# MLP weight sums made early and kept in HBM, and seven products in the first piece's second column group

## The chip, the cores and the metric

The kernel runs on one core of a Trainium2 chip. A core has a matrix engine, TensorE (PE), and three engines for the rest: VectorE (DVE), ScalarE (ACT) and GpSimd (POOL). Each takes its instructions in the order in which they stand in its queue. SyncE (SP) and POOL issue the transfers between HBM and the core's memory. The metric is the time of one execution on the device in microseconds (us); lower is better.

## What is computed

One layer of a decoder trunk, on 256 tokens with 16 meta tokens ahead of them, model width 2048, all in float32:

```python
u = rms_norm(h, g_pre_mix[l])
proj = u @ w_in[l]                       # 2048 x (1024 + 1024 + 1024 + 2048 + 2048)
z_pool, v_conv, g_conv, gate_a, gate_b = jnp.split(proj, splits, axis=-1)
y_a = causal_multiscale_pool(z_pool, w_pool_grp[l], pool_scale[l]) @ w_pool_out[l]
y_b = conformer_conv(v_conv, g_conv, w_dw[l], b_dw[l], conv_ln_g[l], conv_ln_b[l]) @ w_conv_out[l]
m = jax.nn.sigmoid(gate_a) * y_a + jax.nn.sigmoid(gate_b) * y_b
h = h + rms_norm(m @ w_o[l], g_post_mix[l])
u = rms_norm(h, g_pre_mlp[l])
f = jnp.square(jax.nn.relu(u @ w_up[l])) @ w_down[l]     # 2048 -> 8192 -> 2048
h = h + rms_norm(f, g_post_mlp[l])
return h[:, N_META:]
```

The convolution is a causal depthwise one with 31 taps, followed by a layer norm over channels and a swish.

## The kernel before

**Weights.** Every weight matrix passes once from HBM, in chunks of 1 MB: 128 partitions by 2048 float32. A chunk is split into a high part, a cast on ACT (`hi`, line 276), and a low part, a subtraction on DVE (`lo`, line 279). Each product is then three matmuls: high by high, high by low, low by high. Three buffers stand behind the raw chunks and three behind the parts. `fetch()` hands the next chunk to PE; before that it opens the chunks up to two ahead (its load on SP, then its cast and subtraction), and it flushes what was put off for ACT (`late`).

**Stages.** The order of the program is: the start, with x loaded in blocks (`x_in`) that PE transposes (line 434); the projection by w_in, which first makes the convolution's value and gate (to about 107 us), then the pool's input z (to 153 us), then the two gates (16 chunks each, to 327 us; matmuls at line 839); the pool and convolution outputs; w_o; and the MLP from about 505 us to the end. While PE works on w_in, DVE makes the 240 tap steps of the convolution (line 559), which `drain` puts between the chunks by a fixed budget of time for each. The gates' sigmoids are written by ACT (line 868) into two tiles `sg`, one for each gate, in rooms with the tags `s0` and `s1`. The room `s1` holds z before that. POOL has little to do: it sets some constants at the start and, between 377 and 390 us, brings sums of w_o blocks with four loads (`early_sums`, line 921), two of which add to what stands in the core's memory.

**The MLP.** It runs in 8 pieces of 1024 hidden columns (NP = 8). In each, w_up's product is made (steps `U`: half h, pair a or b, part 0 or 1), then relu and square, and then w_down's product, whose weights are 2 by 4 blocks: two halves of the hidden columns by four column blocks of 512. The blocks B11, B12, B21, B22 are the first column group, X1 to X4 (Y in the last piece) the second. For two halves of tokens, two halves of hidden columns and two column blocks, eight block products would be needed; the steps P1 to P7 (first group) and Q1 to Q7 (second group) do with seven, each on a sum or difference of activations (`forms`) and a sum of weight blocks. One block product is 12 matmuls of 128x512. In the first piece's second group the steps X1 to X4 make the eight plain products; in the last piece all sixteen are plain.

Weight sums come in two ways. A load on POOL can add to what stands in a buffer (a *bring*, line 1603): before P1 it adds B12 to B11, at `add:P` it adds B22 to B12 for P7, and likewise in the second group. Or DVE adds two raw buffers in place (line 1598): for P6, P4, Q6 and Q4.

**The order of the MLP.** The strings of steps fix the order on PE and with it the order of loads on SP. The class `Plan` lists the work of all engines with a cost each (a bring on POOL 5.5 us, and 4.0 more until its data are there) and orders ACT, DVE and POOL by when PE needs what they make. The step R makes the row sums of a diagonal (`diag`, line 1638) from which `rb`, the tokens' scale, is copied (line 1923); activations of the first piece (line 1690) and `u` itself (line 1653, four pieces) are scaled by it.

Of the kernel before, what the change touches and what calls it, by code (L numbers as in the profile page):

```python
# [8 lines left out]
F32 = mybir.dt.float32  # L9
# [6 lines left out]
P = 128  # L16
CK = 4
CW = 512
# [97 lines left out]
def hybrid_block(ctx: ExitStack, tc: tile.TileContext, ins: dict, out: bass.AP):  # L116
    nc = tc.nc
    x = ins["x"][0]
    meta = ins["meta"]
    T, D = x.shape  # L120
    M = meta.shape[0]
    L = M + T
    NT = T // P
# [9 lines left out]
    w_down = ins["w_down"][0]  # L133
# [10 lines left out]
    big = ctx.enter_context(tc.tile_pool(name="big", bufs=1))  # L144
# [147 lines left out]
    def split_pieces(c):  # L292
        while opened[c][2]:
            opened[c][2].pop(0)()

    def fetch(ahead=2):

        for c in range(ahead + 1):
            if c == len(opened) and at["n"] < len(stream):
                open_chunk()  # L300
            if c < len(opened):
                split_pieces(c)
        flush()
        return opened.pop(0)[:2]
# [360 lines left out]
    def tap_columns():  # L665
# [194 lines left out]
    def block(n):  # L860
        return slice(n * CW, (n + 1) * CW)
# [4 lines left out]
    def evac_gate(b, n):  # L866
        def f(t, acc):
            late.append(lambda: nc.scalar.activation(sg[b][:, t, block(n)], acc, AF.Sigmoid,
                                                     scale=sc["r"][:, t:t + 1]))
        return f  # L870

    for b in range(2):
        sg[b] = big.tile([P, NT, D], F32, tag=f"s{b}", name=f"sg{b}")
        for n in range(NB):
            project_t(u_of, KD, evac_gate(b, n), f"gate{b}{n}", fill=2.9)

# [594 lines left out]
    plan = Plan()  # L1471
    FIRST_PIECE = "U1a0 U1a1 U1b0 R U1b1"
    PIECE = "U1b1"
    PLAIN = "X3 P1 U0a0+ X1 U0a1+ X4 U0b0+ U0b1+ U1a0+ P5 add:P P6 U1a1+ P3 X2 P7 U1b0+ P4 P2"
    BLOCKS = "P1 U0a0+ U0a1+ Q1 P5 P6 add:P P3 P7 P2 P4 Q5 U0b0+ U0b1+ Q3 Q6 add:Q U1a0+ U1a1+ Q7 U1b0+ Q2 Q4"
    MODES = [PLAIN] + [BLOCKS] * (NP - 2)
    LAST_PIECE = "Y1 U1b1 X1 Y3 Y2 Y4 X2 X3 X4"
    steps = []
    for i in range(NP):
        text = ((FIRST_PIECE if i == 0 else PIECE) + " " + MODES[i] if i < NP - 1 else  # L1480
                LAST_PIECE)
        steps += [(s[:-1], i + 1) if s[-1] == "+" else (s, i) for s in text.split()]
# [4 lines left out]
    col_halves = [slice(h * HALF_CW, (h + 1) * HALF_CW) for h in range(2)]  # L1487
    RAW_OF = {"P1": "B11", "P5": "B11", "P6": "B11", "P4": "B11", "P3": "B22", "P7": "B12",
              "P2": "B21", "Q1": "X1", "Q5": "X1", "Q6": "X1", "Q4": "X1", "Q3": "X4",
              "Q7": "X3", "Q2": "X2"}  # L1490
# [240 lines left out]
    def into_forms(h, pr, i, s_name, box):  # L1731
        G, A, ks = forms[h], f"A{h}{pr}", slice(2 * pr, 2 * pr + 2)

        n = 2 if h or i == NP - 1 or "X1" in MODES[i] else 1

# [128 lines left out]
    def product_block(m_, s, i):  # L1864
        h, f = FORM[s]
        bank = bank_of(s)
        start = s[1] in "65" or bank not in begun and bank != "zq2"
        begun.add(bank)
# [237 lines left out]
```

## Time and profile before

| | |
|---|---|
| median of 3 runs | 1184.26 us (1184.18 to 1184.5) |
| span of the profiled execution | 1183.2 us |
| PE busy | 1172.7 us |
| DVE busy | 1012.7 us |
| ACT busy | 680.7 us |
| POOL busy | 46.9 us |
| HBM read, written | 267.68 MB, 4.19 MB |
| mean rate of the transfers | 231 GB/s |

The profiled execution gives its span, from its first instruction to its last; the times of the runs are 1 us longer than that span. A row of the timeline names the start, the busy time, the engine, the line, the operation, what it writes and reads, the shape, how many instructions there are, and in brackets the idle time of the engine ahead of it with what ended that. A window row gives the busy time of each engine in a stretch. A row of the chain of waits gives start, length, and what ran.

### The profile page before, as it was taken

The page shows a single profiled execution, that of the slowest core. Times are in us where ns is not written, and L with a number is a line of the kernel's source. Part 1 is how long each engine was busy: PE and PEld are TensorE (multiplying, and loading weights), DVE is VectorE, ACT ScalarE, POOL GpSimd, SP SyncE. Part 2 cuts the span into 40 slices and gives each one's busy share as a digit, 9 for nine tenths or more (in the row PEclk, how much of TensorE's full clock was granted, in tenths as well). Part 3 has the DMA queues.
Part 4 walks back from the last instruction along what each step waited for, and adds up shares of the span by engine and source line. Part 5 has one row for each costly group of instructions (what it writes and reads, how often), then busy time and mean ns, then how long its engine had stood idle before and what let it go on. Part 6 is the DMA issues. An engine that isn't in the chain of part 4 may idle for free.

```text
span 1183.2 us, 15773 instructions
## 1 busy us (share of the span) xinstructions
PE 1172.7 (99%) x6351; PEld 1019.0 (86%) x6351; DVE 1012.7 (86%) x1094; ACT 680.7 (58%) x691; POOL 46.9 (4%) x52
## 2 busy tenths in 40 slices
PE   9999999999999999999999999999999999999996
PEld 9999988888888888898888888888888888888886
DVE  6899989986665799987998988989989989889865
ACT  6543344445654466756566766666756667666642
POOL 1000000000000001000001001000000010010000
PEclk9999999999999999999999999999999999999999
DMA  8655555655556967859868899898998998998861
GB/s 295 214 178 179 185 199 186 197 195 183 183 203 228 269 215 221 290 166 318 252 210 238 232 293 232 249 276 226 281 294 220 264 276 230 280 244 249 288 214 72
DMA packets 177882, 272.91 MB, mean 231 GB/s; under 512 B 4657, under 2 KB 92785, under 8 KB 176912
## 3 DMA queue, kind: packets, MB, share of 16 engines
q1 hardware_dynamic: 160176, 235.95, 58.8%
q0 software_dynamic: 16736, 34.76, 16.3%
q10 hardware_dynamic: 896, 1.19, 0.3%
q8 instruction: 50, 0.82, 0.3%
q14 instruction: 24, 0.20, 0.0%
HBM read 267.68 MB, written 4.19 MB: 230 GB/s over the span
## 4 chain that ended last, share of the span: by engine, by line
PE 99%; DMA 0%; DVE 0%; SPq 0%; issue 0%; DVEq 0%; ACT 0%; ACTq 0%
PE bank_u L498 18%; PE acc_gate L839 15%; PE bank_a L1802 10%; PE bank_u L504 9%; PE acc_up L1802 8%; PE bank_b L1802 7%; PE o_c L1185 6%; PE acc_z L493 4%; PE acc_co L839 4%; PE acc_po L839 4%; PE acc_v L493 3%; PE acc_g L493 3%; PE acc_vg L493 2%; PE acc_up L498 1%; PE bank_u L1802 1%; PE o_b L1185 1%
## 5 line engine op out<-in xcount | busy, mean ns | idle before, releaser
L498 PE MATMUL bank_u<-m,hi 128*128 128x512 f32 x960 | 329.4, 390 | 0.0
L504 PE MATMUL bank_u<-m,lo 128*128 128x256 f32 x960 | 265.5, 277 | 0.0
L276 ACT CAST hi<-raw 128x2048 fp32r<-128x2048 f32 (+2 forms) x94 | 151.1, 1620 | 187.2 <-PE acc_gate L839 37.6
L279 DVE TENSOR_TENSOR lo<-raw,hi 128x2048 fp32r<-128x2048 f32 (+2 forms) x94 | 180.2, 1927 | 60.5 <-ACT hi L276 60.1
L498 PEld LDWEIGHTS bank_u<-m,hi 128*128 128x128 f32 x960 | 180.2, 188 | 37.9
L1585 DVE TENSOR_TENSOR lo<-raw_m,hi 128x2048 fp32r<-128x2048 f32 x70 | 160.3, 2289 | 31.8 <-ACT hi L1581 31.7
L504 PEld LDWEIGHTS bank_u<-m,lo 128*128 128x128 f32 x960 | 180.3, 188 | 1.4
L1581 ACT CAST hi<-raw_m 128x2048 fp32r<-128x2048 f32 x70 | 133.9, 1913 | 74.2 <-DVE raw_m L1598 21.3
L839 PE MATMUL acc_gate<-hi,u_um 128*128 128x512 f32 x416 | 131.1, 389 | 0.0
L559 DVE SCALAR_TENSOR_TENSOR c<-a,taps,c 128x256 f32<-128x256 f32 x240 | 98.8, 485 | 0.1
L1802 PE MATMUL bank_a<-hi,forms 128*128 128x512 f32 (+1 forms) x288 | 93.6, 386 | 0.0
L839 PEld LDWEIGHTS acc_gate<-hi,u_um 128*128 128x128 f32 x416 | 78.1, 188 | 16.1
L839 PE MATMUL acc_gate<-lo,u_um 128*128 128x512 f32 x208 | 80.9, 389 | 0.0
L1581 ACT CAST hi<-raw_a 128x2048 fp32r<-128x2048 f32 x29 | 55.4, 1910 | 35.3 <-PE bank_u L498 13.8
L1585 DVE TENSOR_TENSOR lo<-raw_a,hi 128x2048 fp32r<-128x2048 f32 x29 | 66.4, 2289 | 10.8 <-ACT hi L1581 10.7
L1581 ACT CAST hi<-raw_c 128x2048 fp32r<-128x2048 f32 x27 | 51.5, 1908 | 27.3 <-PE bank_u L498 11.8
L1585 DVE TENSOR_TENSOR lo<-raw_c,hi 128x2048 fp32r<-128x2048 f32 x27 | 61.8, 2288 | 5.2 <-ACT hi L1581 5.1
L1802 PEld LDWEIGHTS bank_a<-hi,forms 128*128 128x128 f32 x288 | 53.9, 188 | 11.0
L1585 DVE TENSOR_TENSOR fourth_pair<-raw_m,fourth_pair 128x2048 fp32r<-128x2048 f32 x26 | 59.5, 2288 | 4.4 <-ACT fourth_pair L1581 4.4
L1665 ACT COPY half<-bank_u 128x256 f32<-128x256 f32 x60 | 22.2, 371 | 65.7 <-PE bank_u L504 65.7
L1802 PE MATMUL acc_up<-hi,forms 128*128 128x512 f32 x176 | 57.4, 390 | 0.0
L1802 PE MATMUL bank_a<-lo,forms 128*128 128x512 f32 (+1 forms) x144 | 55.6, 386 | 0.0
(421 smaller groups left out, 2268.2 us busy)
## 6 DMA issues: line engine op xcount, KB each, us to landing
raw<-in_w_in_dram SPq DMA_DIRECT2D x52, 1024.0 KB, 5.0
raw_m<-in_w_down_dram SPq DMA_DIRECT2D x38, 1024.0 KB, 6.8
raw_m<-in_w_down_dram POOLq DMA_DIRECT2D x22, 1024.0 KB, 10.2
raw_a<-in_w_up_dram SPq DMA_DIRECT2D x20, 1024.0 KB, 6.2
raw_c<-in_w_up_dram SPq DMA_DIRECT2D x19, 1024.0 KB, 7.2
raw_m<-in_w_up_dram SPq DMA_DIRECT2D x19, 1024.0 KB, 6.5
raw_a<-in_w_down_dram SPq DMA_DIRECT2D x13, 1024.0 KB, 6.9
raw_c<-in_w_down_dram SPq DMA_DIRECT2D x13, 1024.0 KB, 7.3
```

The source lines that it names most:

```text
L276: nc.scalar.copy(hi[:, sl, cs], raw[:, sl, cs])
L279: nc.vector.tensor_sub(lo[:, sl, cs], raw[:, sl, cs], f32(hi[:, sl, cs]))
L493: nc.tensor.matmul(acc, w[:, k[0], cs], act[:, k[1], a, off:], start=first and n == 0, stop=last and n == 2)
L498: nc.tensor.matmul(acc.rearrange("p (a t) -> p a t", a=2)[:, :, ts], hi[:, k[0], cs], act[:, k[1], :, off + ts.start:off + ts.stop], start ...
L504: nc.tensor.matmul(acc[:, :T], lo[:, k[0], cs], act[:, k[1], 0, off:], start=False, stop=stop, skip_group_check=True)
L559: nc.vector.scalar_tensor_tensor(c, conv["a"][:, q, i:i + T], taps[:, q, i:i + 1], c, op0=ALU.mult, op1=ALU.add)
L839: nc.tensor.matmul(acc, act(kk)[:, a_, ts_], w_[:, k, :], start=kk == 0 and n == 0, stop=kk == nk - 1 and n == 2)
L1185: nc.tensor.matmul(acc, form(k, a_), box[w_][:, k, :], start=start and k == 0 and n == 0, stop=stop and k == CK - 1 and n == 2, skip_group ...
L1581: nc.scalar.copy(box["hi"], raw)
L1585: nc.vector.tensor_sub(box["lo"], raw, f32(box["hi"]))
L1665: nc.scalar.copy(box[j], accs[j][:, :T])
L1802: nc.tensor.matmul(acc, forms[h][:, f, k, a_, :], box[w_][:, k, cs], start=start and k == 0 and n == 0, stop=stop and k == KH - 1 and n == ...
```

## The change

**Seven sums made early.** A generator, `second_sums`, takes a room of two chunks, loads the blocks B12 and B22 of a piece into it with two loads on POOL, adds them on DVE three fetches later and stores the sum with POOL in HBM (`early_t`). Every `fetch` first runs its next step. Pieces 0 to 3 use the room `s0` from the first fetch on, one piece every five fetches; pieces 4 to 6 use the room `s1`, in the gate stage, one every four. The tile of a gate's sigmoids is now made when the first of them is put off, in the same rooms, once the generator has run out. In the MLP, P7's weights are then a plain load from `early_t`.

**Seven sums by adding transfers.** `add:P` now adds B21 to B11 for P4, by a bring, where a DVE sum stood. In all there are 28 brings rather than 26, and 21 DVE sums rather than 26.

**Seven products in the first piece.** Its second group runs Q1 to Q7 instead of X1 to X4. That is one block product of 12 matmuls fewer.

**Another order of the steps.** R stands one up product earlier, and the strings of the pieces are new: one for the first piece, one for odd and one for even pieces, one for the last.

```diff
+    EARLY_SUMS = 7
+    early_t = dram.tile([P, EARLY_SUMS, CK * CW], F32, name="early_t")
+    beside = []
+    def second_sums(tag, pieces, gap):
+        room = big.tile([P, 2, CK * CW], F32, tag=tag, name=f"second_{tag}")
+        for i in pieces:
+            for h in range(2):
+                nc.gpsimd.dma_start(room[:, h].rearrange("p (k c) -> p k c", k=CK),
+                                    columns(w_down, (2 * i + h) * CK, CK, CW)[0][0])
+            yield from [None] * 3
+            nc.vector.tensor_add(room[:, 0], room[:, 0], room[:, 1])
+            nc.gpsimd.dma_start(early_t[:, i], room[:, 0])
+            yield from [None] * gap
+    def beside_step():
+        if beside and next(beside[0], True):
+            beside.pop(0)
     def fetch(ahead=2):
+        beside_step()
...
+    beside.append(second_sums("s0", range(0, 4), 2))
     pending += [(0, after_first), LATER, (0, tap_columns)]
...
     def evac_gate(b, n):
         def f(t, acc):
+            if sg[b] is None:
+                while beside:
+                    beside_step()
+                sg[b] = big.tile([P, NT, D], F32, tag=f"s{b}", name=f"sg{b}")
...
     for b in range(2):
-        sg[b] = big.tile([P, NT, D], F32, tag=f"s{b}", name=f"sg{b}")
         for n in range(NB):
+            if (b, n) == (0, 2):
+                beside.append(second_sums("s1", range(4, EARLY_SUMS), 1))
...
-    FIRST_PIECE = "U1a0 U1a1 U1b0 R U1b1"
-    PLAIN = "X3 P1 U0a0+ X1 U0a1+ X4 U0b0+ U0b1+ U1a0+ P5 add:P P6 U1a1+ P3 X2 P7 U1b0+ P4 P2"
-    BLOCKS = "P1 U0a0+ U0a1+ Q1 P5 P6 add:P P3 P7 P2 P4 Q5 U0b0+ U0b1+ Q3 Q6 add:Q U1a0+ U1a1+ Q7 U1b0+ Q2 Q4"
-    LAST_PIECE = "Y1 U1b1 X1 Y3 Y2 Y4 X2 X3 X4"
+    FIRST = ("U1a0 U1a1 R U1b0 P1 U1b1 Q1 U0a0+ U0a1+ U0b0+ U0b1+ P5 U1a0+ P6 P3 P7 P2 Q5 "
+             "add:Q add:P P4 Q3 Q6 U1a1+ Q2 Q7 U1b0+ Q4")
+    ODD = ("U1b1 P1 U0a0+ U0a1+ P5 Q1 P2 U0b0+ P6 P3 add:P P7 U0b1+ Q5 add:Q P4 Q3 U1a0+ Q6 "
+           "U1a1+ Q7 Q2 Q4 U1b0+")
+    EVEN = ("P1 U1b1 U0a0+ U0a1+ Q1 P5 P6 add:P P2 P3 P7 Q5 P4 U0b0+ U0b1+ U1a0+ Q6 add:Q Q3 "
+            "Q2 U1a1+ Q7 U1b0+ Q4")
+    LAST = ("U1b1 Y1 Y3 X1 Y2 Y4 X2 X3 X4")
...
-    SUM_FOR = {"P6": ("B11", "B22"), "P4": ("B11", "B21"), "Q6": ("X1", "X4"), "Q4": ("X1", "X2")}
-    BRINGS = {"P1": ("B11", "B12"), "Q1": ("X1", "X3"), "add:P": ("B12", "B22"),
+    SUM_FOR = {"P6": ("B11", "B22"), "Q6": ("X1", "X4"), "Q4": ("X1", "X2")}
+    BRINGS = {"P1": ("B11", "B12"), "Q1": ("X1", "X3"), "add:P": ("B11", "B21"),
...
+        if what == "T7":
+            return early_t[:, i].rearrange("p (k c) -> p k c", k=CK), (CK, CW)
```

Three places show how the instructions move.

POOL at the start of the program, before (what an instruction waits for stands in brackets):

```order
L383 MEMSET rows_of 128x32
L385 AFFINE_SELECT rows_of<-rows_of 128x32 [waits Pool_49] x2
L674 MEMSET a 128x8x14 [waits DMAHW1_49,PE_49,Activation_49]
L921 DMA early_sums<-in_w_o_dram 128x4x512 [waits DVE_49,PE_49]
L921 DMA early_sums<-in_w_o_dram 128x4x512
```

and now:

```order
L404 MEMSET rows_of 128x32
L406 AFFINE_SELECT rows_of<-rows_of 128x32 [waits Pool_49] x2
L305 DMA second_s_537<-in_w_down_dram 128x4x512 x2
L695 MEMSET a 128x8x14 [waits DMAHW1_49,PE_49,Activation_49]
L309 DMA early_t<-second_s_537 128x2048 [waits DMASW6_49,DMASW0_49,DVE_49]
L305 DMA second_s_537<-in_w_down_dram 128x4x512 [waits DMASW1_49,DMASW0_49]
```

The first two loads wait for nothing and stand ahead of a MEMSET; the next store waits for its sum, and the loads behind it for the store.

DVE in w_in's stage, at the third of the seven sums (`second_s`; `lo` are the chunks' low parts, `c` the taps), before:

```order
L279 TENSOR_TENSOR lo_1342<-raw_1340,hi_1341 128x2048
L586 TENSOR_TENSOR a<-v_1174,g_99 128x272
L586 TENSOR_TENSOR a<-v_1204,g_99 128x272
L559 SCALAR_TENSOR_TENSOR c<-a,taps,c 128x256 x8
L279 TENSOR_TENSOR lo_1408<-raw_1406,hi_1407 128x2048
```

and now:

```order
L279 TENSOR_TENSOR lo_1354<-raw_1352,hi_1353 128x2048
L607 TENSOR_TENSOR a<-v_1184,g_100 128x272
L607 TENSOR_TENSOR a<-v_1214,g_100 128x272
L580 SCALAR_TENSOR_TENSOR c<-a,taps,c 128x256 x8
L308 TENSOR_TENSOR second_s_537<-second_s_537 128x2048
L279 TENSOR_TENSOR lo_1422<-raw_1420,hi_1421 128x2048
```

One addition stands ahead of a low part; the rest of the order is the same.

DVE in the first MLP piece, from the copy of the scale on (`m` is u being scaled, `raw_m`, `raw_a` and `raw_c` are weight buffers), before:

```order
L1923 COPY rb<-bank_b 128x256
L1690 SCALAR_TENSOR_TENSOR F_raw<-F_raw,rb 128x512 x2
L1585 TENSOR_TENSOR lo_4785<-raw_m_4547,hi_4763 128x2048
L1752 TENSOR_TENSOR forms_4541<-F_raw,forms_4541 128x2x2x128 x2
L1653 TENSOR_TENSOR m<-m,rb 128x2048 x2
L1585 TENSOR_TENSOR lo_4843<-raw_m_4548,hi_4826 128x2048
L1672 TENSOR_TENSOR F_raw<-half_0_4806,bank_u_4549 128x256
L1672 TENSOR_TENSOR F_raw<-half_0_4828,bank_u_4550 128x256
L1653 TENSOR_TENSOR m<-m,rb 128x2048
L1585 TENSOR_TENSOR lo_4881<-raw_a,hi_4857 128x2048
```

and now:

```order
L1953 COPY rb<-bank_b 128x256
L1720 SCALAR_TENSOR_TENSOR F_raw<-F_raw,rb 128x512 x2
L1615 TENSOR_TENSOR lo_4779<-raw_m_4577,hi_4755 128x2048
L1782 TENSOR_TENSOR forms_4572<-F_raw,forms_4572 128x2x128 x2
L1720 SCALAR_TENSOR_TENSOR F_raw<-F_raw,rb 128x512
L1743 TENSOR_TENSOR F_raw<-F_raw 128x256
L1683 TENSOR_TENSOR m<-m,rb 128x2048
L1615 TENSOR_TENSOR lo_4823<-raw_m_4578,hi_4818 128x2048
L1683 TENSOR_TENSOR m<-m,rb 128x2048
L1615 TENSOR_TENSOR lo_4864<-raw_m_4579,hi_4842 128x2048
...
L1683 TENSOR_TENSOR m<-m,rb 128x2048
L1615 TENSOR_TENSOR lo_4921<-raw_a,hi_4878 128x2048
```

The forms of the first half are now single, as in the other pieces; a third activation row block is scaled and differenced ahead of the rescaling of u; and the last row shown makes the weights of U0a1.

More of the change, by code (lines that the diff above doesn't have):

```diff
@@ L872, in hybrid_block @@
     for b in range(2):
-        sg[b] = big.tile([P, NT, D], F32, tag=f"s{b}", name=f"sg{b}")
         for n in range(NB):
+            if (b, n) == (0, 2):
+                assert not beside
+                beside.append(second_sums("s1", range(4, EARLY_SUMS), 1))
             project_t(u_of, KD, evac_gate(b, n), f"gate{b}{n}", fill=2.9)
@@ L1487, in hybrid_block @@
     col_halves = [slice(h * HALF_CW, (h + 1) * HALF_CW) for h in range(2)]
[L1488 removed]
+    RAW_OF = {"P1": "B11", "P5": "B11", "P6": "B11", "P4": "B11", "P3": "B22", "P7": "T7",
               "P2": "B21", "Q1": "X1", "Q5": "X1", "Q6": "X1", "Q4": "X1", "Q3": "X4",
               "Q7": "X3", "Q2": "X2"}
[L1491 to L1493 removed]
+    SUM_FOR = {"P6": ("B11", "B22"), "Q6": ("X1", "X4"), "Q4": ("X1", "X2")}
+    BRINGS = {"P1": ("B11", "B12"), "Q1": ("X1", "X3"), "add:P": ("B11", "B21"),
               "add:Q": ("X3", "X4")}
@@ L1866, in product_block @@
         bank = bank_of(s)
-        start = s[1] in "65" or bank not in begun and bank != "zq2"
+        start = s[1] in "65" or bank not in begun
         begun.add(bank)
```

7 lines of the change are left out of this document (2 added, 5 removed).

## The prediction

> **What bounds the kernel now.** I read the page's head first, then the chain that ended last, then windows, and only then the rows at the places that the change touches. The page's length, its busy times and its shares of the chain:
>
> ```profile
> span 1183.2 us, 15773 instructions
> PE 1172.7 (99%) x6351; PEld 1019.0 (86%) x6351; DVE 1012.7 (86%) x1094; ACT 680.7 (58%) x691; POOL 46.9 (4%) x52
> PE 99%; DMA 0%; DVE 0%; SPq 0%; issue 0%; DVEq 0%; ACT 0%; ACTq 0%
> ```
>
> TensorE (PE) is busy 1172.7 of 1183.2 us and is 99% of the chain. So time saved on another engine is worth nothing by itself, a matmul saved is worth its whole duration, and anything that comes late for PE is paid in full, since nothing on PE can catch up. The median of the runs, 1184.26, is 1.06 above this span; I carry that 1.06 through unchanged and add differences to 1184.26.
>
> Windows show how much cover the other engines have (the columns are PE, PE load, DVE, ACT and POOL busy, the granted clock, the DMA share and GB/s):
>
> ```profile
> 0.00:50.00 50.00, 48.53 (x379) 47.23 (x380) 35.74 (x80) 34.35 (x62) 4.84 (x18) 1.00 0.78 259
> 50.00:100.00 50.00, 50.00 (x407) 50.00 (x407) 50.00 (x84) 17.79 (x15) 0.00 (x0) 1.00 0.58 190
> 100.00:150.00 50.00, 50.00 (x417) 50.00 (x416) 49.90 (x89) 18.89 (x13) 0.00 (x0) 1.00 0.58 189
> 150.00:200.00 50.00, 50.00 (x233) 41.92 (x232) 44.05 (x58) 21.61 (x17) 0.00 (x0) 1.00 0.58 190
> 650.00:700.00 50.00, 50.00 (x255) 42.63 (x255) 47.63 (x38) 34.22 (x31) 1.27 (x1) 1.00 0.91 250
> ```
>
> PE is full everywhere but at the start. VectorE (DVE) is full as well from 50 to 150 us: idle 0.10 us out of 100. From 150 on it has some 6 us in 50. In the MLP it has 2.4 in 50 and the DMA engines 9% to spare. Three of the places that the change touches are thus the tight ones: the start, the stage where DVE is full, and the MLP.
>
> **Term 1, the product that goes.** The first MLP piece's second column group takes seven products where eight block products stood. In the chain of the MLP one product is 12 matmuls:
>
> ```profile
> 655.92 2.72 PE bank_b L1802 x12
> ```
>
> One fewer: **-2.72 us**, on PE itself, so the whole of it counts. The five DVE sums that go (26 to 21, 2.29 each, 11.4 us) and the changed order of the steps save nothing, because PE waits for DVE nowhere in the MLP.
>
> **Term 2, two loads at the start.** The helper's first step runs in the first fetch of weights, and its two 1 MB loads on POOL wait for nothing, so they are issued as soon as POOL has come to them, right behind the two selects. Rows of the timeline, of the windows, and of the DMA issues (line, KB, us to landing):
>
> ```profile
> 5.23 0.50 POOL L385 TENSOR_SCALAR_AFFINE_SELECT rows_of<-rows_of 128x32 f32<-128x32 f32 x2
> 4.82 0.37 SPq L353 DMA_DIRECT2D x_in<-in_x_dram  x1
> 12.19 0.63 PE L434 MATMUL xt<-ident,x_in 128*128 128x128 f32 x4
> 5.00:10.00 5.00, 4.65 (x39) 4.20 (x38) 3.69 (x10) 3.05 (x8) 0.72 (x5) 1.00 0.97 293
> 10.00:15.00 5.00, 5.00 (x39) 4.67 (x38) 3.57 (x8) 3.31 (x9) 0.00 (x0) 1.00 1.07 384
> 15.00:20.00 5.00, 5.00 (x44) 5.00 (x43) 3.95 (x9) 2.82 (x8) 0.00 (x0) 1.00 1.08 386
> x_in<-in_x_dram SPq DMA_DIRECT2D x1, 512.0 KB, 7.2
> raw<-in_w_conv_out_dram SPq DMA_DIRECT2D x2, 1024.0 KB, 5.2
> raw<-in_w_conv_out_dram SPq DMA_DIRECT2D x1, 1024.0 KB, 8.5
> ```
>
> The loads go out at about 5.7 us into DMA engines that run at 0.97 to 1.08 of their time until 20 us. The second block of x is issued at 4.82, lands 7.2 later at 12.0, and PE transposes it at 12.19: its slack is 0.1 to 0.2. What two POOL loads of 1 MB do to an SP load is seen in the last two rows: alone the loads from w_conv_out land in 5.2, the one issued beside the two POOL loads of `early_sums` takes 8.5, so 3.3 longer. 3.3 less 0.1 of slack is **+3.2 us**. The bounds are 0, if the x blocks pass first, and the whole volume ahead of them, 2.10 MB / 386 GB/s = 5.4. I take 3.2, since its row is the same pair of loads beside the same kind of load.
>
> **Term 3, four sums on a full DVE.** Pieces 0 to 3 put a 128x2048 addition on DVE ahead of the low-part subtractions of w_in's chunks 9, 14, 19 and 24. The duration comes from the MLP's own sums, the pitch from two successive starts, the slack from when PE first reads the low part of chunks 24 and 26:
>
> ```profile
> L1598 DVE TENSOR_TENSOR raw_m<-raw_m,raw_m x10: 2284/2286/2292, 594.9 to 1106.7; 128x2048 f32<-128x2048 f32 x10
> 143.40 2.31 DVE L279 TENSOR_TENSOR lo<-raw,hi 128x2048 fp32r<-128x2048 f32 x1
> 153.11 0.39 PE L839 MATMUL acc_gate<-lo,u_um 128*128 128x512 f32 x1
> 155.05 2.29 DVE L279 TENSOR_TENSOR lo<-raw,hi 128x2048 fp32r<-128x2048 f32 x1
> 157.25 0.69 DVE L724 TENSOR_TENSOR sums<-z 128x514 f32<-128x514 f32 x1
> 163.99 0.39 PE L839 MATMUL acc_gate<-lo,u_um 128*128 128x512 f32 x1
> ```
>
> A 2.29 us instruction holds DVE for 2.2 (155.05 to 157.25). Four make 8.8; idle time takes up 0.1 of it. Chunk 24's low part ends at 143.40 + 2.31 = 145.71 and is read at 153.11: slack 7.4. Chunk 26's ends at 157.34 and is read at 163.99: slack 6.65, the smallest behind all four. 8.8 - 0.1 - 6.65 = **+2.0 us**. Bounds: 0, if DVE gets ahead of PE (below), and 2.4, if the pitch is the full 2.29. The stores and loads between them have five chunks for each sum, 27 us at the 5.44 between those two reads' chunks ((163.99 - 153.11) / 2), and are hidden.
>
> **Term 4, three more sums in the gate stage.** DVE has room here (44.05 of 50), so the sums themselves cost nothing. But the room of pieces 4 to 6 is where the second gate's sigmoids are written, and the first of these must wait until the last store has read it. Behind it in ACT's queue stand the high parts of the next chunks, and behind those DVE's low parts and PE:
>
> ```profile
> 258.39 2.29 DVE L279 TENSOR_TENSOR lo<-raw,hi 128x2048 fp32r<-128x2048 f32 x1 [0.83 <-ACT hi L276]
> 263.74 1.25 ACT L868 ACTIVATE sg<-acc_gate,r_in 128x512 f32<-128x512 f32 x2
> 267.37 1.92 ACT L276 CAST hi<-raw 128x2048 fp32r<-128x2048 f32 x1 [2.37 <-issue]
> 269.31 2.29 DVE L279 TENSOR_TENSOR lo<-raw,hi 128x2048 fp32r<-128x2048 f32 x1
> 278.49 0.39 PE L839 MATMUL acc_gate<-lo,u_um 128*128 128x512 f32 x1
> L921 POOL DMA_DIRECT2D early_sums<-in_w_o_dram x4: 776/1042/1306, 377.3 to 388.7; - x4
> DMA to landing us min/median/max: 7.5/11.3/17.1
> ```
>
> The last sum stands ahead of the subtraction at 258.39, so its store goes out near 260. No POOL store is in this trace; the nearest are POOL's four loads into `early_sums`, which land 7.5 to 17.1 after issue, median 11.3. By the median the sigmoid starts at 271.3 rather than 263.74, 7.6 late. The low part of 269.31 ends at 271.60, 6.89 before PE reads it, and 2.37 of idle time ahead of the cast gives way as well. With the first slack alone the stall is 0.7, with both none. At 17.1 it is 6.5 or 4.1. I take **+0.5 us**, with 0 and 4 as ends.
>
> **Term 5, the MLP's new order.** Rows of the first piece (chain, then DVE):
>
> ```profile
> 535.92 0.23 PE bank_u L498
> 536.27 0.23 PE bank_u L498
> 543.61 0.48 DVE L1638 TENSOR_SCALAR diag<-ident,p 128x128 fp32r<-128x128 f32 x2
> 549.38 0.43 DVE L1923 COPY rb<-bank_b 128x256 f32<-128x256 f32 x1 [1.22 <-PE bank_b L480]
> 549.84 1.29 DVE L1690 SCALAR_TENSOR_TENSOR F_raw<-F_raw,rb 128x512 f32<-128x512 f32 x2
> 554.54 4.49 DVE L1653 TENSOR_TENSOR m<-m,rb 128x2048 fp32r<-128x2048 f32 x2
> ```
>
> An up product is 16 pairs of matmuls at a pitch of 0.35, so 5.60. The step R (row sums) comes one up product earlier: the copy to `rb` at 549.38 - 5.60 = 543.78. The diagonal that R reads ends at 544.09 in this profile, but the squares ahead of it now stand together on ACT, so it is ready sooner; if not, R costs about 0.6. After R, PE runs two up products, P1, Q1 and another up product before U0a1: 3 x 5.60 + 2 x 2.72 = 22.2. DVE needs, from the copy to U0a1's low part, 0.46, three row scalings of 0.65, four rescalings of u and four low parts at 2.2, and five small ones of about 0.33: 21.7. It is 0.5 ahead: **0 us**, with 1.5 as the upper end if R is late as well as the chain.
>
> In the later pieces the weights of P4 now are a transfer that adds B21 into B11 where a DVE sum stood, and P7's come summed from HBM. Landing times of the adding transfers:
>
> ```profile
> L1603 POOL DMA_DIRECT2D raw_m<-in_w_down_dram x22: 1257/1271/1815, 553.7 to 1083.8; - x22
> DMA to landing us min/median/max: 8.4/9.6/13.9
> ```
>
> In an even piece, P6 to P4 is five products, 13.6 us, less 4.2 for P4's own cast and subtraction: 9.4 for the transfer, and what the split of P6 ran ahead of PE. In an odd one it is 12.3. At the median of 9.6 that is enough: 0. (The rival below takes the slow end.)
>
> **Sum:** -2.72 + 3.2 + 2.0 + 0.5 + 0 = +2.98, so 1184.26 + 2.98 = **1187.2 us**. With each term at its low end but the first: 1181.5; the likeliest case's own range is 1185 to 1190.
>
> **Rivals.** A change under 0.2%, 2.4 us, can't be told from none, so the bounds are 1181.9 and 1186.6.
>
> - *All terms arrive* (A): 1187.2, chance 0.43.
> - *The start hides the loads* (B): if x's blocks, issued 0.9 us earlier, keep their turn in the DMA engines, 3.2 goes: 1184.0. For it: x_in is already in flight. Against it: the w_conv_out load of 8.5 us. 0.17.
> - *DVE gets ahead* (C): if PE is late by 3.2 from the start while DVE is not, PE's lateness gives chunk 26 a slack of 9.85, and 8.8 no longer reaches it: 1185.2. Against it: DVE's idle time in the first 50 us is mostly spent waiting for PE and loads, so it should be late too. 0.12.
> - *Only the product counts* (D, the other side): loads hidden and the sums swallowed, because the fixed order leaves the low parts three buffers ahead: 1184.26 - 2.72 = 1181.5. It decides where the x block is less than 0.1 late and chunk 26's slack exceeds 8.7. 0.15.
> - *Adding transfers land late* (E): at 13.9 us an even piece would be short by 13.9 - 9.4 = 4.5, an odd one by 1.6; over three of each 18. If one in four lands so, +4.5: 1191.7. For it: the DMA share of 0.91 in the MLP, and 28 adding transfers rather than 26. 0.08.
> - *A slower clock after the gap* (F): if a gap of 3.2 us at 12 us made PE run at half speed for as long again, +1.6: 1188.8. Against it: the granted clock is 1.00 in every window, the first included, which has idle time at its head. 0.05. [...]
>
> Faster is D, 0.15; the same B and C, 0.29; slower A, E and F, 0.56. The range leaves out D and the far part of E: 1182.8 to 1191.0.
>
> **What would show it.** Term 2: a wait of about 3 us of PE for x_in near 12 us, at the transposes, and an x_in landing above 10 us. Term 3: PE idle before a low-part matmul between 150 and 170 us, released by DVE, with DVE without idle time up to there. Term 4: ACT idle before the first sigmoid of the second gate, released by a DMA, and a short PE wait near 278. Term 1: 6339 PE instructions rather than 6351. Term 5: PE idle ahead of P4 or U0a1. The prediction is wrong if PE has no wait at 12 us (B or D), or if there is one and the w_in stage has none (C).

## The result, and the profile after

The changed kernel takes 1198.16 us (median of 4 runs, 1197.93 to 1198.61) against 1184.38 us for the kernel before on the same chip: a ratio of 1.0115, 95% interval 1.0101 to 1.0129. It is slower, as forecast, but by 13.8 us instead of 2.8, and the time lies 7 us above the range.

The head of the page and PE's row:

```profile
span 1196.1 us, 15786 instructions
PE 1178.7 (99%) x6339; PEld 1020.3 (85%) x6339; DVE 1021.7 (85%) x1101; ACT 687.3 (57%) x694; POOL 63.6 (5%) x75
```

PE runs 6339 instructions, 12 fewer than before, so the block product did go. Yet PE is *busier*, 1178.7 instead of 1172.7 us. Idle time explains only part of the loss: some matmuls have become slower. The view of what PE waited for (total, times, longest) names the idle part:

```profile
PE bank_u L519 <- DVE F_raw L1702: 2.5, 1, 2.5
PE acc_vg L514 <- ACT hi L276: 1.9, 1, 1.9
PE acc_gate L861 <- DVE lo L279: 1.2, 2, 1.0
PE acc_vg L514 <- DVE lo L279: 0.6, 3, 0.2
PE acc_vg L514 <- ACT u_um L456: 0.6, 1, 0.6
```

`acc_vg` is the start, `acc_gate` with `lo` the stretch behind w_in's stage, `bank_u` the first MLP piece. Windows of the start and of the full-DVE stretch:

```profile
15.00:30.00 15.00, 11.90 (x90) 11.04 (x90) 7.69 (x17) 9.20 (x19) 0.00 (x0) 1.00 1.05 373
150.00:200.00 50.00, 48.80 (x244) 41.16 (x243) 49.86 (x69) 20.57 (x15) 2.05 (x3) 1.00 0.72 250
600.00:1140.00 540.00, 540.00 (x2768) 460.75 (x2767) 479.66 (x393) 350.55 (x309) 31.65 (x25) 1.00 0.90 260
```

The answering windows of before (the second, 150 to 200, is shown ahead of the prediction: PE 50.00, DVE 44.05):

```profile
15.00:30.00 15.00, 15.00 (x126) 15.00 (x125) 11.06 (x22) 10.80 (x24) 0.00 (x0) 1.00 0.87 303
600.00:1140.00 540.00, 540.00 (x2788) 462.37 (x2787) 487.98 (x393) 350.00 (x314) 30.49 (x24) 1.00 0.89 257
```

From 15 to 30 us PE gets through 90 matmuls instead of 126. At 0.124 us each, the pitch of these 272-wide ones, the missing 36 are 4.5 us. From 600 to 1140 us PE is full in both, without a wait, at the same clock, and still does 2768 matmuls rather than 2788.

Pairing each matmul with the same one of before and following how much later it starts gives the whole account of the profiled execution:

| place | us |
|---|---|
| start, to 25 us | +4.4 |
| behind w_in's full DVE (at 129, 159 and 171 us) | +2.1 |
| from there to the end of w_o | 0.0 |
| wait behind R in the first MLP piece | +2.8 |
| half clock behind that wait | +1.65 |
| the product that goes | -2.7 |
| slower matmuls from 566 us to the end | +4.8 |
| sum (spans: 1196.1 - 1183.2 = 12.9) | +13.0 |

### The profile page after: what moved, and what is told of

Read it like the earlier page. It is cut to its first block, busy times and chain, and to the rows that moved or that the text cites. A ratio compares the mean times of both kernels' runs of the same rounds, so it can differ in the third digit from the quotient of the medians.

```text
span 1196.1 us, 15786 instructions
## 1 busy us (share of the span) xinstructions
PE 1178.7 (99%) x6339; PEld 1020.3 (85%) x6339; DVE 1021.7 (85%) x1101; ACT 687.3 (57%) x694; POOL 63.6 (5%) x75
## 4 chain that ended last, share of the span: by engine, by line
PE 85%; DVE 11%; DMA 2%; ACT 1%; issue 1%; SPq 0%; DVEq 0%; ACTq 0%
PE bank_u L519 18%; PE acc_gate L861 14%; PE bank_a L1832 10%; PE bank_u L525 9%; PE acc_up L1832 8%; PE bank_b L1832 7%; PE o_c L1213 5%; DVE c L580 4%; DVE lo L279 4%; PE acc_co L861 4%; PE acc_po L861 4%; PE acc_vg L514 1%; DMA raw<-in_w_in_dram 1%; PE acc_v L514 1%; PE bank_u L1832 1%; DVE second_s L308 1%
## 5 line engine op out<-in xcount | busy, mean ns | idle before, releaser
L519 PE MATMUL bank_u<-m,hi 128*128 128x512 f32 x960 | 334.6, 393 | 2.5 <-DVE F_raw L1702 2.5
L1615 DVE TENSOR_TENSOR lo<-raw_m,hi 128x2048 fp32r<-128x2048 f32 x85 | 194.5, 2288 | 43.1 <-ACT hi L1611 42.6
L1611 ACT CAST hi<-raw_m 128x2048 fp32r<-128x2048 f32 x85 | 162.3, 1909 | 101.5 <-PE bank_u L519 54.5
L1832 PE MATMUL bank_a<-hi,forms 128*128 128x512 f32 (+1 forms) x256 | 82.1, 384 | 0.0
L1832 PE MATMUL bank_b<-hi,forms 128*128 128x512 f32 (+1 forms) x192 | 61.0, 382 | 0.0
L1832 PEld LDWEIGHTS bank_a<-hi,forms 128*128 128x128 f32 x256 | 47.6, 188 | 10.1
L1213 PE MATMUL o_c<-hi,m 128*128 128x512 f32 x160 | 50.8, 390 | 0.0
L1832 PE MATMUL acc_up<-hi,forms 128*128 128x512 f32 x152 | 49.9, 390 | 0.0
L1832 PE MATMUL bank_a<-lo,forms 128*128 128x512 f32 (+1 forms) x128 | 49.2, 385 | 0.0
L861 PEld LDWEIGHTS acc_gate<-lo,u_um 128*128 128x128 f32 x208 | 39.0, 188 | 10.0 <-DVE lo L279 1.9
```

The costliest lines, as they stand in the source:

```text
L519: nc.tensor.matmul(acc.rearrange("p (a t) -> p a t", a=2)[:, :, ts], hi[:, k[0], cs], act[:, k[1], :, off + ts.start:off + ts.stop], start ...
L861: nc.tensor.matmul(acc, act(kk)[:, a_, ts_], w_[:, k, :], start=kk == 0 and n == 0, stop=kk == nk - 1 and n == 2)
L1213: nc.tensor.matmul(acc, form(k, a_), box[w_][:, k, :], start=start and k == 0 and n == 0, stop=stop and k == CK - 1 and n == 2, skip_group ...
L1611: nc.scalar.copy(box["hi"], raw)
L1615: nc.vector.tensor_sub(box["lo"], raw, f32(box["hi"]))
L1832: nc.tensor.matmul(acc, forms[h][:, f, k, a_, :], box[w_][:, k, cs], start=start and k == 0 and n == 0, stop=stop and k == KH - 1 and n == ...
```

## Experiments

### Where the rooms lie

The last line of that account has no counterpart in the prediction. In the chain, an up product's pairs of matmuls start 0.34 us apart in the MLP of before (first fence) and 0.35 apart in parts of the changed kernel (second fence); some block products take 2.75 instead of 2.72:

```profile
675.31 0.23 PE bank_u L498
675.65 0.23 PE bank_u L498
```

```profile
651.72 0.23 PE bank_u L519
652.07 0.23 PE bank_u L519
607.65 2.75 PE bank_a L1832 x12
```

Between 600 and 1140 us, 18 of 50 up products take 5.60 us instead of 5.45, and 67 of 95 block products more than 2.73; before, none and 34 of 95. Those 34 all stand directly behind an up product, a place where a block product takes about 2.75 in either kernel; of the others, 31 of 59 are slow now and none of 62 before. The new order of the steps was one candidate. The other came from the built program's memory: a room gets its place when it is first asked for. Before, z asks for `s1` first; now the helper asks for `s0` first, and the two rooms have changed places. With that the data of `forms_0`, which PE reads as stationary operand in half the block products, begin at byte 113856 of a partition instead of 130304, that is 192 bytes behind a multiple of 256 instead of on one. Those of `forms_1` begin on a multiple both times.

In the changed kernel, `s1` is asked for first again:

```diff
+    big.tile([P, NT, D], F32, tag="s1", name="s1_first")
     beside.append(second_sums("s0", range(0, 4), 2))
```

> The changed kernel with the room s1 asked for ahead of s0, so that both lie at the addresses that they had before (forms_0 at 130304, forms_1 64 bytes behind 113856). Theory: the matmuls of the MLP that are some ns slower each (an up product 5.60 rather than 5.45 us, many block products 2.75 rather than 2.72) are so because the rooms have changed places: -4.8 us, 1193.4, and up products at 5.45. Rival: the new order of the steps makes them slower: 1198, and 5.60 stays.

Measured: 1192.28 us, 5.9 under the changed kernel (ratio to before 1.0064, 1.0049 to 1.0079). No up product between 600 and 1140 us takes 5.60 any more. The profiled execution, at 1190.55 us the shortest of the four, is 7.4 us shorter than that of the changed kernel: 3.8 of it are the matmuls between 600 and 1150 us and 1.3 those ahead of them in the MLP, 0.7 came at the start, and 1.5 from the clock, which did not fall in it (below).

The other direction, in the kernel before, with nothing else changed:

```diff
+    big.tile([P, NT, D], F32, tag="s0", name="s0_first")
     pending += [(0, after_first), LATER, (0, tap_columns)]
```

> The kernel before, with the room s0 asked for ahead of s1, which swaps the addresses of the two rooms as in the changed kernel, and nothing else. If the rooms' addresses slow the matmuls: 1184.4 + 4 to 5 = 1189, with up products of 5.60 us in the MLP. Rival, the order of the steps: 1184.4, no change.

Measured: 1189.0 us against 1184.49, ratio 1.0038 (1.0023 to 1.0053). The window of 540 us, which is full, holds 2773 matmuls instead of 2788, and 18 up products of 5.60. Of the 61 block products that do not stand directly behind an up product 28 are slow; the one shown second took 2.72 in the kernel before (third line):

```profile
600.00:1140.00 540.00, 540.00 (x2773) 461.11 (x2772) 485.82 (x390) 346.49 (x310) 30.48 (x24) 1.00 0.90 255
620.94 2.75 PE bank_a L1803 x12
620.44 2.72 PE bank_a L1802 x12
```

So the addresses alone make it, and the order of the steps does not. To tell the begin of the data from the place of the rooms, the swapped kernel was given back its alignment only, by moving the 64 bytes that led `forms_1` to `forms_0`:

```diff
-        room = big.tile([P, b * LINE + KD * T], F32R, tag=f"s{b}", name=f"forms_{b}")
-        forms.append(room[:, b * LINE:].rearrange(...))
+        room = big.tile([P, (1 - b) * LINE + KD * T], F32R, tag=f"s{b}", name=f"forms_{b}")
+        forms.append(room[:, (1 - b) * LINE:].rearrange(...))
```

> The kernel before with its two rooms swapped, as in the run that measured 1189.0, but with the 64 bytes of lead that forms_1 has in its room given to forms_0 instead. Then the data of both forms begin at multiples of 256 bytes again (113920 and 130304), in rooms that have still changed places. In the swapped run forms_0 began 192 bytes behind such a multiple. Theory: the begin of forms_0 modulo 256 bytes makes the slower matmuls: back to 1184.5 to 1185. Rival: the rooms' places as such: 1189.

Measured: 1183.99 us against 1184.45, ratio 0.9997 (0.9987 to 1.0006), with the rooms still swapped:

```profile
600.00:1140.00 540.00, 540.00 (x2788) 462.26 (x2787) 487.68 (x393) 349.27 (x313) 30.50 (x24) 1.00 0.89 257
```

2788 matmuls again, no up product of 5.60, and none of those block products slow. `forms_1` begins at the same address as in the swapped kernel, so of what PE reads in the MLP only `forms_0` has moved, by 64 bytes, from 113856 to 113920. With its begin 192 bytes behind a multiple of 256 the window of 540 us held 2773 matmuls, with its begin on one 2788. The up products do not read `forms_0` themselves, and yet 18 of them took 5.60 instead of 5.45 us. How the one slows the other was not tried, and that begin is not all that sets the pace of an up product: the first four of the MLP take 5.60 in the kernel before, where both forms begin on a multiple, and 5.45 in this run. The w_o stage agrees: its `forms_o`, which PE reads from the begin of the room `s0`, lies 192 bytes off in this run too, and its 96 matmuls take 22.0 us here and in the swapped and the changed kernel, against 21.8 in the kernel before.

### The start

The first run moved the helper's first step five fetches later in the program:

```diff
-    def second_sums(tag, pieces, gap):
+    def second_sums(tag, pieces, gap, wait=0):
+        yield from [None] * wait
...
-    beside.append(second_sums("s0", range(0, 4), 2))
+    beside.append(second_sums("s0", range(0, 4), 2, 5))
```

> The helper's first loads come five fetches later, behind the start; its four sums in w_in's stage move on by five chunks (14, 19, 24 and 29 instead of 9 to 24), nothing else. If the two loads at the start cost what the first 25 us show (4.4 us of PE), the time falls from 1198.2 to 1193.8, and to 1191.7 if the 2.1 us of waits for DVE near 130 to 170 us go too, since one sum fewer lies ahead of chunk 26. Rival: the start is late for another reason (the new place of the instructions): no change, 1198.

Measured: 1198.37 us, no change. POOL's timeline shows why:

```profile
5.67 0.19 POOL L695 MEMSET a<- 128x112 f32 x1
6.11 1.58 POOL L305 DMA_DIRECT2D second_s<-in_w_down_dram  x2 [0.25 <-issue]
```

The loads wait for nothing, and POOL has nothing else to do: five fetches later in the program is 0.45 us later on POOL (5.66 in the changed kernel). The run tells nothing on the price of the loads. But it moved the four sums, and the waits for DVE moved with them: 0.6 near 185 us and 1.5 at 274, where there had been 2.1 at 129 to 171. The start itself was 1.2 us worse in this profile, with the clock at half from 23 to 26 us.

A held start needs something to wait for. Here DVE writes one column of the room in a later fetch, with the rooms at their old places:

```diff
+        if tag == "s0":
+            yield from [None] * 6
+            nc.vector.memset(room[:, :, 0:1], 0.0)
         for i in pieces:
```

> The changed kernel with both rooms at their old addresses, and with the first loads of the room s0 held back by a real dependency: DVE writes one column of the room in the seventh fetch of the helper's count, and only then can POOL load into it. The place in the program alone held back nothing (the loads of the run with the late start went out at 6.11 us). Theory: the waits of the first 30 us (about 3 to 4 us) are the two loads' doing and go: 1192.3 - 3.5 = 1188.8; the waits for DVE near 160 us may shrink too, 1187.5. Rival: the start is late for other reasons: 1192.

Measured: 1192.3 us, as without the hold. The page shows both that the start's cost is gone and what took its place:

```profile
15.00:30.00 15.00, 15.00 (x126) 15.00 (x125) 10.74 (x22) 10.91 (x24) 0.00 (x0) 1.00 0.85 291
75.01 1.57 POOL L308 DMA_DIRECT2D second_s<-in_w_down_dram  x2 [69.15 <-DVE second_s L305]
PE cs_m L504 <- DVE cs_lo_m L785: 2.6, 1, 2.6
PE acc_gate L865 <- DVE lo L279: 2.3, 2, 1.4
```

126 matmuls from 15 to 30 us, as before the change. But the seven additions now come when DVE has no room at all: PE waits for DVE at 192, 248 and 273 us, and the same matmuls are 5.5 us later there than before. The hold also moved the four sums some 30 us later, but the run with the late start has them at the same places (the first at 91.8 us there, 91.7 here): with its start 5.6 us late they cost it 2.1, and here, with the start in time, 5.5. What PE loses at the start thus gives DVE a lead. The two costs are not a sum; part of the one hides the other.

The sums alone, in the kernel before, with the rooms at their old places and nothing that reads the sums:

> The kernel before with the early sums alone (loads, additions, stores), which nothing reads, and both rooms at their old addresses. Theory: the start costs 3.4 to 4.4 us and the waits for DVE in w_in's stage 2.1, the gate stage nothing: 1184.5 + 5.5 to 6.5 = 1190 to 1191. Rival: without the changed MLP the sums hide better: below 1188.

Measured: 1190.64 us against 1184.57, ratio 1.0049 (1.0034 to 1.0064). 4.5 us at the start and 2.1 behind w_in's stage in its profile, and none of the helper's waits anywhere else: the price of the sums is independent of the MLP.

What was late at the start is not x_in but w_in's first chunks. ACT's timeline of the changed kernel, and the DMA issues from 5.6 to 7.4 us (KB, us to landing):

```profile
12.66 0.47 ACT L456 ACTIVATE u_um<-xt,vecs 128x256 fp32r<-128x256 f32 x1 [1.69 <-PE xt L455]
18.03 0.62 ACT L276 CAST hi<-raw 128x512 fp32r<-128x512 f32 x1 [3.65 <-DMA raw<-in_w_in_dram]
second_s<-in_w_down_dram POOLq DMA_DIRECT2D x2, 1024.0 KB, 11.4
raw<-in_w_in_dram SPq DMA_DIRECT2D x3, 256.0 KB, 13.1
```

The block of x is read at 12.66 without delay; the cast at 18.03 has waited 3.65 us for a weight load of 256 KB that took 13.1. Without the helper, in the profile of before, the three such loads issued from 5.6 to 7.4 us took 7.5. The next block of x, issued at 8.09, took 13.6 as well, but it was in time; only in the run with R later (below) does PE wait for a block of x too, 0.9 us.

### The first MLP piece

The MLP's part alone; P7's weights are loaded from B12 without B22 added, so these products are not those of the reference:

```diff
-    beside.append(second_sums("s0", range(0, 4), 2))
-                beside.append(second_sums("s1", range(4, EARLY_SUMS), 1))
-            return early_t[:, i].rearrange("p (k c) -> p k c", k=CK), (CK, CW)
+            return columns(w_down, (i * 2) * KH, KH, CW)[0]
```

> The MLP's part of the change alone: no early sums, no rooms for them, and P7's weights are loaded plainly from B12, so the addition of B22 to them is left out. The rooms then lie as before. Theory: -2.7 for the product, +2.5 for the wait behind R, and +1.7 where the clock falls after it: 1184.3 to 1186.0, with no wait of PE outside of the MLP's start. Rival: the new order loses elsewhere in the MLP too (transfers that land late): 1188 or more.

Measured: 1185.1 us against 1184.57, ratio 1.0004 (0.9994 to 1.0013): the same. The ten executions took 1183.7 to 1184.1 us where the mean granted clock was 0.997 (five of them), and 1186.1 to 1187.4 where it was 0.995 to 0.996 (five, the profiled one among them). In the profile one wait is left, 2.0 us behind R, and the clock falls behind it (windows of 1 us; PE busy is the second number, the granted clock the third from the right):

```profile
545.00:546.00 1.00, 0.00 (x0) 0.00 (x0) 1.00 (x3) 1.00 (x1) 0.00 (x0) 1.00 0.92 340
547.00:548.00 1.00, 1.00 (x5) 0.90 (x4) 1.00 (x3) 0.57 (x1) 0.47 (x1) 0.50 0.66 232
549.00:550.00 1.00, 1.00 (x4) 0.87 (x4) 1.00 (x1) 0.88 (x3) 0.00 (x0) 0.50 0.90 161
```

The same in the changed kernel:

```profile
551.00:552.00 1.00, 0.00 (x0) 0.00 (x0) 1.00 (x1) 1.00 (x1) 0.00 (x0) 1.00 0.84 322
555.00:556.00 1.00, 1.00 (x5) 0.90 (x4) 1.00 (x1) 1.00 (x3) 0.00 (x0) 0.50 0.92 108
556.00:557.00 1.00, 1.00 (x4) 0.81 (x4) 1.00 (x2) 0.72 (x3) 0.00 (x0) 0.50 1.08 190
```

-2.7 for the product, +2.1 for the wait and 1.65 for the clock leave +1.1 in the profile: what the product saves is spent in the same piece. Where the mean clock was 0.997 the fall may not have come; none of those executions was profiled. Outside of it the new order loses nothing, so the adding transfers are in time.

The wait's own account, in DVE's timeline of the changed kernel:

```profile
542.45 0.16 DVE L1655 TENSOR_REDUCE tot<-ssq 128x2 f32<-128x8 f32 x1 [3.62 <-ACT ng_offset=None)_3_1_4641 L1050]
544.25 2.29 DVE L1615 TENSOR_TENSOR lo<-raw_a,hi 128x2048 fp32r<-128x2048 f32 x1 [1.43 <-ACT hi L1611]
550.23 2.28 DVE L1615 TENSOR_TENSOR lo<-raw_c,hi 128x2048 fp32r<-128x2048 f32 x1
552.44 0.75 DVE L1702 TENSOR_TENSOR F_raw<-half,bank_u 128x256 f32<-128x256 f32 x2
552.90 0.50 PE L519 MATMUL bank_u<-m,hi 128*128 128x512 f32 x1 [2.50 <-DVE F_raw L1702]
```

With R earlier, the planner puts DVE's mean (`tot`) ahead of the low parts, and DVE idles 3.62 us for ACT's squares. All behind it is late: the low part of P1's weights stands ahead of the totals of U1a, and U1b0 cannot overwrite their banks. The planner does not see this: it takes ACT and DVE as free when the plan begins, while ACT's last cast ahead of it, which waited 2.08 us for a load, ends at 536.4.

R one up product later, where it stood:

```diff
-    FIRST = ("U1a0 U1a1 R U1b0 P1 U1b1 Q1 ..."
+    FIRST = ("U1a0 U1a1 U1b0 R P1 U1b1 Q1 ..."
```

> The changed kernel with the step R one up product later, where it stood before (U1a0 U1a1 U1b0 R P1 instead of U1a0 U1a1 R U1b0 P1). Theory: the 2.5 us in which PE waits for DVE's totals of U1a, behind R, come from DVE's order, which the early R has changed, and the half clock for 3.4 us after it from that gap: both go, -4.3 us, 1193.9. Rival 1: the gap is the price of the new order as a whole and turns up at another step: 1198. Rival 2: only the gap goes and the clock falls anyway: 1195.7.

Measured: 1201.44 us (ratio 1.0141, 1.0124 to 1.0158), 3.3 slower still. Rival 1 held, and worse. DVE's mean stands behind the first low part again, as before the change, and still the wait behind U1a stays (1.86), and a second one comes at P1, whose activations now come too late:

```profile
552.28 0.50 PE L519 MATMUL bank_u<-m,hi 128*128 128x512 f32 x1 [1.86 <-DVE F_raw L1702]
561.40 0.80 PE L1832 MATMUL acc_up<-hi,forms 128*128 128x512 f32 x1 [3.15 <-ACT forms L1780]
```

R's place is therefore not the cause by itself. ACT's late begin was tested next, with three of its eight squares made ahead of the last casts:

```diff
+    ssq2 = const.tile([P, NT, NB], F32, name="ssq2")
+    for n in range(3):
+        square_of(h1[:, 0, block(n)], ssq2, 0, n)
     hi, lo = fetch()
...
     for t in range(NT):
         for n in range(NB):
+            if t * NB + n < 3:
+                continue
             plan.add("ACT", 0.75, square_h1(t, n), reads=("h1",), writes=("junk", "ssq2"))
```

> The changed kernel with three of the eight squares of h1 (ACT, 0.75 us each) made ahead of the last chunk's casts, where ACT waits 2.1 us for a load, instead of in the MLP's plan. The plan takes every engine as free when it begins; in the profile ACT is busy with the last cast until 536.4, 2.9 us past its begin, and the squares end at 542.4, with DVE's mean, rsqrt, diagonal and the totals behind them. Theory: the wait of 2.5 us behind R is made by that lateness of ACT, and the half clock by the wait; with 2.25 us less work on ACT both go: 1198.2 - 4 = 1194. Rival: DVE has too much to do there whatever ACT does: the wait moves to another step, 1198.

Measured: 1193.15 us (ratio 1.0074, 1.0059 to 1.009), 5.0 under the changed kernel. PE waits nowhere in the MLP, and the clock stays:

```profile
550.00:600.00 50.00, 50.00 (x274) 43.10 (x273) 49.13 (x46) 35.23 (x41) 2.94 (x3) 1.00 0.87 238
```

2.25 us of ACT's work, moved by some us into time in which ACT idled, cost 2.5 us of PE and the clock behind it.

### All together

Both rooms as before, the squares ahead, and the sums by transfers alone, so that DVE has nothing to add:

```diff
-    def second_sums(tag, pieces, gap):
+    def second_sums(tag, pieces, wait):
+        yield from [None] * wait
         room = big.tile([P, 2, CK * CW], F32, tag=tag, name=f"second_{tag}")
+        nc.vector.memset(room[:, 0, 0:1], 0.0)
         for i in pieces:
-            for h in range(2):
+            for h, op in enumerate(({}, {"accum_op": ALU.add})):
-                nc.gpsimd.dma_start(room[:, h]...
+                nc.gpsimd.dma_start(room[:, 0]..., **op)
-            yield from [None] * 3
-            nc.vector.tensor_add(room[:, 0], room[:, 0], room[:, 1])
             nc.gpsimd.dma_start(early_t[:, i], room[:, 0])
-            yield from [None] * gap
+            yield
```

> All causes taken away together: both rooms at their old addresses; the early sums made by transfers alone (a load, an adding load, a store, one after the other), with no addition on DVE, from the third fetch of the helper's count on and held by a written column; the three squares ahead. Theory: only the product that goes is left: 1184.4 - 2.7 = 1181.7, under the kernel before, if no wait is left at the start, in w_in's stage and behind R. Rival: the transfers beside w_in's loads make these late (18 MB more in 200 us): 1184 to 1188, with waits of PE for chunks between 60 and 250 us.

Measured: 1187.3 us (ratio 1.0023, 1.0014 to 1.0032), neither of the two. No chunk of w_in is late, so the rival falls. One wait is left, where it had not been expected: three sums in `s1` are one too many. The last store goes out at 267.2, and the second gate's first sigmoid waits for it:

```profile
267.22 0.57 POOL L309 DMA_DIRECT2D early_t<-second_s  x1 [11.28 <-DMA second_s<-in_w_down_dram]
276.23 1.27 ACT L895 ACTIVATE sg<-acc_gate,r_in 128x512 f32<-128x512 f32 x2 [12.40 <-DMA early_t<-second_s]
281.67 0.79 PE L862 MATMUL acc_gate<-lo,u_um 128*128 128x512 f32 x1 [1.83 <-DVE lo L279]
```

PE idles 0.92 and 1.83 us, and the clock falls again for three us behind it: 4.3 in all.

Five sums in `s0`, begun two fetches sooner, and two in `s1`:

```diff
-    beside.append(second_sums("s0", range(0, 4), 3))
+    beside.append(second_sums("s0", range(0, 5), 1))
-                beside.append(second_sums("s1", range(4, EARLY_SUMS), 0))
+                beside.append(second_sums("s1", range(5, EARLY_SUMS), 0))
```

> The run before this with five sums in the room s0 and two in s1 instead of four and three, and begun two fetches sooner (its hold on DVE at about 42 us). There the last of three sums in s1 was stored at 267.2, and the second gate's first sigmoid, the casts behind it and PE waited: 2.7 us of PE at 278, and 1.6 more by half clock. Theory: with two sums that store goes out near 243, 20 us ahead of the sigmoid, and all of that 4.3 goes: 1187.3 - 4.3 = 1183.0, 1.5 to 2 us under the kernel before. Rival: five sums in s0 are too many, its last store lands behind 176 us and the same wait turns up at the first gate: 1186 to 1187.

Measured: 1182.87 us (11 runs, 1182.33 to 1183.31) against 1184.55, ratio 0.9986, interval 0.9977 to 0.9995. It is faster than both kernels, 15.3 us under the changed one. The last store goes out at 243.75, and the list of PE's waits holds only the one at the program's head, which every run has:

```profile
243.75 0.57 POOL L309 DMA_DIRECT2D early_t<-second_s  x1 [11.64 <-DMA second_s<-in_w_down_dram]
PE idle L415 <- DVE rb L329: 1.1, 1, 1.1
```

Not all of the product's 2.7 us arrives: in the profiles of this run and of the one before it the matmuls from the end of w_o to the last are 1.9 us shorter than in the kernel before. In this one part of the rest lies in the first piece, where six up products take 5.60 to 5.95 us instead of four; why is not known.

## Why the prediction was wrong

| step | predicted | measured |
|---|---|---|
| Term 1, a product less | -2.72 | -2.7 |
| Term 2, loads at the start | +3.2 (0 to 5.4) | +4.4 |
| Term 3, sums on a full DVE | +2.0 (0 to 2.4) | +2.1 |
| Term 4, sigmoids behind the store | +0.5 (0 to 4) | 0 |
| Term 5, the first piece | 0 (0 to 1.5) | +2.8 and +1.65 by the clock |
| not in the sum: begin of `forms_0` | - | +4.8 |

**Right:** that it gets slower, Terms 1 and 3, and the mechanism of Term 2. Term 3 was right to 0.1 us, but with luck, because the start was late as well: with the start held and the sums some 30 us later, they cost 5.5. Rival C, which said that lateness at the start gives DVE a lead, was seen in that way after all; I had given it 0.12 and taken the two terms as a plain sum.

**Term 2** named the wrong victim and was 1.2 too small. I looked for the transfer with the smallest slack, x_in, and priced one load beside two. But behind x_in stand the 256 KB loads of w_in's first chunks, which were in time only as long as the two loads did not run beside them (as in the run that held these back); some took 13.1 us, and PE waited for several of them, between 14.8 and 22.3 us and not at 12, where the prediction had looked for its sign. The bound from volume, 5.4, held.

**Term 4** overpriced the store: with no store in the trace I took POOL's loads into `early_sums`, 11.3 us. The stores into `early_t` held up POOL's next load by 4.3 to 5.7 us, and they landed 4.4 to 7.8 us after issue, median 5.9. ACT did idle 2.70 us ahead of the second gate's first sigmoid, which began at 273.21: the last store had gone out at 268.60 and landed 4.5 later (the view names a row of DVE that ended at the same time). No wait of PE followed; PE was 6.5 us later there than before, and that may have been the cover. The mechanism itself is real: in the run with three sums in `s1` the store went out at 267.2, the sigmoid could begin at 276.2, and that cost 4.3 us.

**Term 5** is the step that failed. "It is 0.5 ahead: 0 us" was worked out from the copy to `rb` on, as if DVE came to it with nothing behind. I did not follow DVE and ACT from the plan's begin, where ACT's squares, moved together, hold DVE's mean, and the mean holds two low parts and the totals. I even noted the moved squares, as a gain for the diagonal. The diagonal was indeed ready in time (R started 0.1 late); what was late was what had been pushed behind it.

**Rival F** had the right price (+1.6, measured 1.65) and the wrong place: the half clock did not follow a wait at 12 us but the one of 2.5 us that Term 5 had missed. Its "for as long again" was assumed; the clock was 0.50 for 3.41 us, from 554.28 to 557.69.

**The largest miss** is not a term at all. The diff shows that a tile is asked for earlier and another later; that this exchanges two rooms' addresses, and that 192 bytes of begin matter to matmuls 500 us later, was in no row that I read. The bounds came from the terms, so no bound could hold it. Rows did show that the same up product exists at two paces: 5.60 us, which I quoted from the first piece, and 5.45 in the rest of the MLP. I took the first for all and did not ask why they differ.

## What to carry to other kernels

Compare the addresses that two builds give to their tiles, not only the order of their instructions: here a room asked for earlier moved another, and the kernel became 0.4% slower (1189.0 against 1184.49 us) with PE full from 15 to 1140 us in both. The place of an instruction in the program alone delayed little on the idle queue: the loads, which waited for nothing, went out 0.45 us later for five fetches (6.11 against 5.66 us). And two lateness costs on one path must not be added without asking whether the first gives cover to the second. When a step is moved earlier, follow every engine from where its queue last ran dry, with what it still owes, instead of from the step itself.

## What the hardware showed that was not expected

- With the data of `forms_0`, a stationary operand of PE, 192 bytes behind a multiple of 256 bytes rather than on one, the MLP was slower: by 3.8 us between 600 and 1150 us in the profile of the changed kernel against that with the rooms back, by up to 0.03 us for a product of 12 and by 0.15 for an up product, which reads other operands. Of what PE reads in the MLP, only that begin differs between the two runs of 1189.0 and 1183.99 us. No other begin was tried.
- PE's granted clock fell to half (0.50 in windows of 1 us) for about 3.4 us (6.8 in the run with R later) after idle stretches of 2.0 us (the MLP's part alone), 2.5 (the changed kernel) and 0.92 with 1.83 (three sums in `s1`), in these three at a cost of 1.6 to 1.7. After 2.4 us it fell in the run with the held start, and in the run with the rooms back it did not:

```profile
550.00:551.00 1.00, 0.00 (x0) 0.00 (x0) 1.00 (x1) 1.00 (x1) 0.00 (x0) 1.00 0.91 330
553.00:554.00 1.00, 1.00 (x8) 0.87 (x7) 1.00 (x3) 0.92 (x2) 0.12 (x1) 1.00 0.69 179
```

  So the length of the gap alone does not decide; where it lies may. In the changed kernel the clock falls at 554.28, is full again at 557.69, 3.41 us later, and next changes, to half, at 1189.16, that is 185 times 3.413 us after. Cut its profile at such places into stretches of 3.413 us: PE idles 2.04 and 2.06 us in the two ahead of the falls, and at most 1.64 in any other up to the second fall. Ahead of falls in other runs such a stretch has 1.97 us without PE's work in the MLP's part alone, 2.21 with three sums in `s1` and 2.44 with the held start. With the rooms back the gap is split over two, 1.48 and 0.91 us. No run moved a gap and nothing else, so a rule is not shown.
- An adding load and a store beside w_in's loads, at a DMA share of 1.02 from 50 to 150 us in the fastest version, made no chunk late. From 15 to 30 us of the changed kernel, at a share of 1.05, two loads cost most of the 4.4 us: the share alone does not tell what a further transfer costs. How far ahead of its use each chunk is loaded may decide it; no run varied that alone.
